# Weight sums issued behind weight slabs, and a down projection streamed by single chunks in a new order

## The chip, the core and the metric

The kernel runs on one core of one Trainium2 chip. The metric is the time of one execution on the device in microseconds. Before the change it is 2502.09 us, the median of three runs (2501.57, 2502.09 and 2509.57).

## What is computed

One layer of a transformer on 2048 tokens of width 1024 in float32: chunked softmax attention with 16 heads, each frame looking at its own 64-frame chunk and the eight before it, and then a SwiGLU network of inner width 2816. Each half is wrapped in two RMS norms.

```python
def rms_norm(x, g):
    xf = x.astype(jnp.float32)
    y = xf * lax.rsqrt(jnp.mean(xf * xf, axis=-1, keepdims=True) + RMS_EPS)
    return (y * g.astype(jnp.float32)).astype(x.dtype)
def swiglu(h, w_gate, w_up, w_down):
    return (jax.nn.silu(h @ w_gate) * (h @ w_up)) @ w_down
...
        h = rms_norm(x, g_pre_mix[i])
            m = chunk_relpos_attention(h, w_qkv[i], w_o[i], rel_bias[i // N_MIXERS])
        x = x + rms_norm(m, g_post_mix[i])
        h = rms_norm(x, g_pre_ffn[i])
        x = x + rms_norm(swiglu(h, w_gate[i], w_up[i], w_down[i]), g_post_ffn[i])
```

## The kernel before

Every float32 operand of a large product is split in two fp32r parts, a high one (ScalarE copies it, L117 and L333) and a low one (VectorE subtracts it, L118 and L334), and each product is three matmuls, high by high, high by low and low by high (L181, L182, L183).

The tokens are worked in two groups of 1024, each of two halves of 512. First come the projections of both groups with the attention between them (0 to 1115 us): weights come as slabs of 2048 columns through `fetch`, one slab ahead of its use, in two pieces of 512 KB through one buffer `raw`. Then come, for each group, gate and up (`gate_up`, 1115 to 1612 us for group 0 and 1835 to 2258 us for group 1) and down (`down`, 1612 to 1835 us and 2258 to 2484 us). These use a fast matrix multiplication in the manner of Strassen and Winograd: seven products of half size instead of eight, on sums of blocks of the activations (B11, T1 and so on) and sums of blocks of the weights (S1 to S4).

The weight sums are made once: `weight_sums` loads four blocks into tiles `ws` (four buffers), makes four additions on VectorE and stores four sums to memory. There are 17 such units, 11 for gate and up and 6 for down. They are put in `later`, a queue of steps that is worked off as the dense matmuls are written: each step has a weight, and each product of three 512-wide matmuls gives one unit of credit; `pause` is a step that does nothing.

TensorE's order is the order in which the program writes its instructions. The order on the other engines and of the DMAs issued by SyncE is set by the framework's scheduler, which may put an instruction ahead of its place in the program when its inputs and a buffer are there.

The down projection takes its operands from a stream: `ffn_ahead` loads and splits items before they are used. An item of down is a pair of the 11 chunks of 256 inner columns (the first stands alone): 512 KB of weights into one of two buffers (`raw_x`, `raw_d`), and for each chunk the activations into a scratch tile (`narrow`, nine in turn); the split activations have four buffers (tag `w4`, shared with the weights of gate and up that are loaded raw), the split weights four (`whi`, `wlo`). Items are loaded two ahead and split one ahead. Each of the seven products of down (`product`) walks all chunks, with four accumulators in PSUM; the order is B11, T1, B21, B22, T2, T3, T4 in both groups. In the last group T4 is worked twice, for 256 tokens each, so that the first half's final norm (`rstd_steps` and `finish`, put in `later` by `ended`) can run beside the second half's matmuls; its weights are loaded and split twice. The final norm of the second half of the tokens (512 wide) is put in `later` after T3, and `finish` adds the residual with eight additions, of which `share` of every four go to VectorE and the rest to GpSimd.

Of the kernel before, what the change touches and what calls it, by code (L numbers as in the profile page):

```python
# [16 lines left out]
P = 128  # L17
# [30 lines left out]
def trunk(  # L48
# [71 lines left out]
    def fetch():  # L120
# [9 lines left out]
        for c in range(2):  # L130
            here = slice(c * 1024, c * 1024 + 1024)
            if n in roomy:
                part = raw[:, here]
            else:
# [4 lines left out]
                sp.dma_start(part, plan[n][:, here])  # L139
            split_part(*tiles[c], part)  # L140
        ready.append(tiles)

    taken = [0]
# [59 lines left out]
    def pause(w):  # L203
        return [(w, lambda: None)]
# [599 lines left out]
    def weight_sums(src, dst):  # L804
# [14 lines left out]
        steps = [(0.5, lambda n=n: load(n)) for n in ("A11", "A21", "A22", "A12")] + pause(6.0)  # L819
        steps += [(2.0, lambda a=a: add(*a)) for a in sums] + pause(4.0)  # L820
# [44 lines left out]
    odd = [0]  # L865

    def down_stream(g, n, cs, c0, cols):

        a = FACTOR[n]
        m = len(cs) * HALF  # L870

        def load():
            odd[0] += 1
            if odd[0] % 2:
                raw = phase["fp"].tile([P, 1024], F32, tag="rawx", name="raw_x", bufs=1)
            else:
                raw = wp.tile([P, 1024], F32, tag="raw", name="raw_d", bufs=1)
            src = w_d[BLOCK_AT[a]] if a in BLOCK_AT else sum_d[a]
            sp.dma_start(raw[:, :m], src[:, cs[0] : cs[0] + len(cs), :].rearrange("p a b -> p (a b)"))
            cols_ = []  # L880
            for c in cs:
                cols_.append(narrow("raw_a")[:, :cols])
                sp.dma_start(cols_[-1], a_d[g][n][:, c, c0 : c0 + cols])
            return raw, cols_

        def make(got):
            raw, cols_ = got
            w = w_tile(f"d{g}_{n}_{cs[0]}_{c0}")
            split_part(w[0][:, :m], w[1][:, :m], raw[:, :m])
            acts = []  # L890
            for r in cols_:
                t = phase["fp"].tile([P, 2, HALF], F32R, tag="w4", name="a", bufs=4)
                split(t[:, 0, :cols], t[:, 1, :cols], r)
                acts.append(t)
            return w, acts

        return load, make, 2, 1


# [91 lines left out]
    def down_order(g):  # L991

        chunks = [[0]] + [[c, c + 1] for c in range(1, NC, 2)]
        for n in ("B11", "T1", "B21", "B22", "T2", "T3", "T4"):
            parts = ((0, HALF),) if n != "T4" or g < NG - 1 else ((0, HALF // 2), (HALF // 2, HALF // 2))
            for c0, cols in parts:
                for cs in chunks:
                    yield n, cs, c0, cols

    def down(g, store, between=lambda n: None):  # L1000

        p = xp.tile([P, 10, HALF], F32, tag="big", name="terms", bufs=1)
        p1, p5 = ([p[:, 4 * n + d, :] for d in range(4)] for n in range(2))

        def four(late):
# [5 lines left out]
        def product(pts, first, after):  # L1011
            for m in range(len(range(0, NC, 2))):
                (hi, lo), acts = ffn_take()
                for d in range(4):
                    for n, a in enumerate(acts):
                        cols = pts[d].shape[-1]
                        w = slice(n * HALF + d * P, n * HALF + d * P + P)
                        products(
                            pts[d], hi[:, w], lo[:, w], a[:, 0, :cols], a[:, 1, :cols],
                            first and m == 0, m == NC // 2 and n == len(acts) - 1, not first,  # L1020
                        )
                        yield 3 * C512 * cols / HALF
                    if m == NC // 2:
                        after(d)
# [428 lines left out]
```

## Time and profile before

| | us |
|---|---|
| median of three runs | 2502.09 |
| the profiled execution's own time | 2500.28 |
| its span, first to last instruction | 2498.4 |
| TensorE matmul busy in it | 2417.9 |
| VectorE busy | 1597.0 |
| ScalarE busy | 1142.5 |
| GpSimd busy | 321.2 |

Busy time of an engine counts the stretches in which at least one of its instructions ran. A wait is the idle time just before an instruction, with the instruction that released it. In the views, PE is TensorE, PEld its weight load, DVE VectorE, ACT ScalarE, POOL GpSimd and SP SyncE, which issues the DMAs; L182 is line 182 of the kernel, and a name such as `pd<-a,whi_d_T` is the output tile and the inputs. PEclk is the granted TensorE clock as a share of 2.4 GHz.

### The profile page before, as it was taken

What the parts mean: (1) busy time and instruction counts of PE and PEld (TensorE: products, weight loads), DVE (VectorE), ACT (ScalarE), POOL (GpSimd) and SP (SyncE); (2) the same over time, 40 slices, a digit from 0 to 9 for tenths busy, and PEclk for the clock granted to TensorE, in tenths of its full rate; (3) what the DMA queues carried; (4) which work ended last, traced back from release to release, by engine and by line L of the source; (5) the groups of instructions that cost most, each with busy time, mean ns of one, the idle gap of its engine ahead of it and who ended that gap; (6) DMA issues with size and microseconds to landing.
All of it is one profiled execution on the core that took longest, in us unless ns stands there. A gap on an engine that the chain in (4) does not pass through costs nothing.

```text
span 2498.4 us, 34441 instructions
## 1 busy us (share of the span) xinstructions
PE 2417.9 (97%) x12620; PEld 1998.1 (80%) x12620; DVE 1597.0 (64%) x2647; ACT 1142.5 (46%) x1930; POOL 321.2 (13%) x422
## 2 busy tenths in 40 slices
PE   7999999999999999999999999999999999999996
PEld 5787878778888888878888788788778888887885
DVE  7877775657665655568566665676556664554557
ACT  5554454654565545555333333355333323334543
POOL 4233232201222222210000000000000000000000
PEclk8999999999999999999999999999999999999998
DMA  6787861445232111147576754477667654457554
GB/s 217 276 294 282 288 238 64 156 159 168 66 100 83 62 53 62 61 137 253 166 239 215 241 178 146 154 238 244 200 204 250 219 172 149 153 180 230 191 160 160
DMA packets 176680, 444.05 MB, mean 178 GB/s; under 512 B 19424, under 2 KB 24304, under 8 KB 175232
## 3 DMA queue, kind: packets, MB, share of 16 engines
q1 hardware_dynamic: 176512, 441.87, 53.5%
q8 instruction: 99, 1.62, 0.3%
q14 instruction: 69, 0.57, 0.1%
HBM read 327.97 MB, written 113.82 MB: 177 GB/s over the span
## 4 chain that ended last, share of the span: by engine, by line
PE 46%; DMA 4%; DVE 3%; issue 2%; ACT 1%; SPq 0%; POOL 0%; DVEq 0%; POOLq 0%; ACTq 0%
PE pd L182 5%; PE pd L183 5%; PE pd L181 5%; PE pb L181 4%; PE pb L183 4%; PE pb L182 4%; PE pa L181 3%; PE pa L183 3%; PE pa L182 3%; PE pc L181 3%; PE pc L183 3%; PE pc L182 3%; DMA y<-y 1%; DMA x<-y 1%; PE mm L181 1%
## 5 line engine op out<-in xcount | busy, mean ns | idle before, releaser
L181 PE MATMUL mm<-hb,whi 128*128 128x512 f32 x720 | 299.5, 416 | 3.3 <-ACT hb L333 3.0
L531 POOL TENSOR_SCALAR sc<-sc,rows 128x640 f32<-128x640 f32 (+4 forms) x256 | 213.2, 838 | 597.6 <-DVE rows L530 561.7
L182 PE MATMUL mm<-hb,whi 128*128 128x512 f32 x720 | 285.4, 396 | 2.8 <-POOL hb L334 1.5
L527 ACT ACTIVATE sc<-sc,nmax 128x640 f32<-128x640 f32 (+4 forms) x256 | 193.8, 758 | 202.3 <-DVE nmax L523 198.0
L183 PE MATMUL mm<-hb,wlo 128*128 128x512 f32 x720 | 285.5, 397 | 0.0
L523 DVE CUSTOM_DVE_ANT_0 sc<-st,bias 128x640 f32<-128x640 f32 (+4 forms) x256 | 180.4, 737 | 82.9 <-PE st L515 76.4
L181 PE MATMUL pb<-hb,whi_gu_T 128*128 128x512 f32 x528 | 206.2, 391 | 3.9 <-DVE terms L948 3.9
L183 PE MATMUL pb<-hb,wlo_gu_T 128*128 128x512 f32 x528 | 205.5, 389 | 0.0
L182 PE MATMUL pb<-hb,whi_gu_T 128*128 128x512 f32 x528 | 205.4, 389 | 0.0
L251 POOL TENSOR_TENSOR rs<-ms,neg_half 128x4 f32<-128x4 f32 (+1 forms) x12 | 17.2, 1431 | 1279.2 <-DVE ms L249 1279.0
L334 DVE TENSOR_TENSOR a<-raw_a,a 128x512 fp32r<-128x512 f32 (+1 forms) x165 | 105.8, 653 | 109.7 <-ACT a L333 109.1
L181 PEld LDWEIGHTS mm<-hb,whi 128*128 128x128 f32 x720 | 137.0, 190 | 38.0 <-issue 14.6
L333 ACT ACTIVATE a<-raw_a 128x512 fp32r<-128x512 f32 (+1 forms) x165 | 96.6, 596 | 145.7 <-PE pd L183 115.3
L183 PEld LDWEIGHTS mm<-hb,wlo 128*128 128x128 f32 x720 | 136.8, 190 | 30.2
L182 PE MATMUL pd<-a,whi_d_T 128*128 128x512 f32 (+1 forms) x396 | 146.8, 371 | 12.7 <-DVE a L334 12.7
L182 PEld LDWEIGHTS mm<-hb,whi 128*128 128x128 f32 x720 | 137.3, 191 | 25.6 <-POOL hb L334 3.2
L181 PE MATMUL pd<-a,whi_d_T 128*128 128x512 f32 (+1 forms) x396 | 146.5, 370 | 2.0 <-ACT a L333 2.0
L183 PE MATMUL pd<-a,wlo_d_T 128*128 128x512 f32 (+1 forms) x396 | 145.8, 368 | 0.0
L181 PE MATMUL mm<-whi,hb 128*128 128x256 f32 x480 | 141.9, 296 | 0.0
L181 PE MATMUL pa<-hb,whi_gu_B 128*128 128x512 f32 x352 | 137.5, 391 | 0.1
L183 PE MATMUL pa<-hb,wlo_gu_B 128*128 128x512 f32 x352 | 137.0, 389 | 0.0
L182 PE MATMUL pa<-hb,whi_gu_B 128*128 128x512 f32 x352 | 137.0, 389 | 0.0
(222 smaller groups left out, 5898.1 us busy)
## 6 DMA issues: line engine op xcount, KB each, us to landing
raw<-gu_S SPq DMA_DIRECT2D x88, 512.0 KB, 3.7
raw<-in_w_gu SPq DMA_DIRECT2D x66, 512.0 KB, 4.0
y<-y SPq DMA_DIRECT2D x96, 256.0 KB, 4.0
ws_A<-in_w_gu SPq DMA_DIRECT2D x44, 512.0 KB, 5.7
gu_S<-ws_A SPq DMA_DIRECT2D x44, 512.0 KB, 3.0
raw<-in_w_a SPq DMA_DIRECT2D x40, 512.0 KB, 4.0
raw_a<-aT SPq DMA_DIRECT2D x77, 256.0 KB, 4.4
aT<-T SPq DMA_DIRECT2D x66, 256.0 KB, 4.1
```

Source lines behind the costliest of these rows:

```text
L181: pe.matmul(pt, a_hi, b_hi, start=first, stop=False, skip_group_check=go_on)
L182: pe.matmul(pt, a_hi, b_lo, start=False, stop=False, skip_group_check=go_on)
L183: pe.matmul(pt, a_lo, b_hi, start=False, stop=last, skip_group_check=go_on)
L251: pool.tensor_tensor(r[0][:, :nb], m[:, :nb], neg_half.to_broadcast([P, nb]), op=ALU.pow)
L333: act.activation(hi, src, AF.Copy)
L334: eng.tensor_tensor(lo, src, hi.bitcast(F32), op=ALU.subtract)
L523: dve.tensor_tensor_reduce(out=sc[:, :n], in0=st[:, c0 : c0 + n], in1=rev, scale=-1.0, scalar=3.0e38, op0=ALU.add, op1=ALU.min, accum_out= ...
L527: act.activation(sc[:, :n], sc[:, :n], AF.Exp, bias=nmax, scale=-1.0, accum_out=rows[:, 0:1])
L531: pool.tensor_scalar(sc[:, :n], sc[:, :n], rows[:, 1:2], 1.0, op0=ALU.mult, op1=ALU.mult)
```

## The change

1. The 17 units of weight sums no longer go through `later`. After the second piece of each slab 3 to 11 (group 0) and 22 to 31 (group 1) has been asked for, `fetch` writes one unit, with its loads and stores held behind that slab's DMA on SyncE's queue (`issue_after`). The pauses inside a unit are gone. So nine units stand in group 0 and eight in group 1.
2. An item of down is one chunk (256 KB of weights, 256 KB of activations, both in scratch tiles), loaded four ahead and split three ahead. The buffers `raw_x` and `raw_d` are gone.
3. In the last group the order is B11, T1, T2, T3, B22, B21, T4. T4 is walked once, 512 wide, for its first seven chunks; the last four chunks are held and worked first for 256 tokens, then for the other 256. The second half's final norm is queued after B22, with half of its additions on GpSimd.
4. Some pauses before norms change, and after the last but one attention job's output no dense work is written before the transposes that follow.

```diff
@@ fetch
-                sp.dma_start(part, plan[n][:, here])
+                ins = sp.dma_start(part, plan[n][:, here])
             split_part(*tiles[c], part)
         ready.append(tiles)
+        if units and n in UNIT_AT:
+            with tc.issue_after(ins.ins):
+                for _, step in units.popleft():
+                    step()
+    UNIT_AT = set(range(3, 12)) | set(range(22, 32))
@@ weight_sums
-        steps = [(0.5, lambda n=n: load(n)) for n in ("A11", "A21", "A22", "A12")] + pause(6.0)
-        steps += [(2.0, lambda a=a: add(*a)) for a in sums] + pause(4.0)
+        steps = [(0.5, lambda n=n: load(n)) for n in ("A11", "A21", "A22", "A12")]
+        steps += [(2.0, lambda a=a: add(*a)) for a in sums]
@@ down_stream
+            raw, cols = narrow("raw_d"), narrow("raw_a")
             src = w_d[BLOCK_AT[a]] if a in BLOCK_AT else sum_d[a]
+            sp.dma_start(raw, src[:, c, :])
+            sp.dma_start(cols, a_d[g][n][:, c, :])
...
-        return load, make, 2, 1
+        return load, make, 4, 3
@@ down, product
+            for m in range(NC - tail):
+                item = ffn_take()
                 for d in range(4):
+                    yield part(item, m, d, whole)
+            items = []
+            for here in parts:
+                for d in range(4):
+                    for m in range(tail):
+                        if len(items) == m:
+                            items.append(ffn_take())
+                        yield part(items[m], NC - tail + m, d, here)
+                    after(d, here)
+                between_parts(here)
@@ down, the last group
+        yield from product(pc, False, c22)
+        if end:
+            yield from product(pb, False, c12)
+            between(0)
+            p2 = four()
+            yield from product(p2, True, lambda d, _: store(0, d, whole, add(p2[d], p1[d])))
+        p4 = four(not end)
         yield from product(
+            p4, True, lambda d, here: store(0, 4 + d, here, add(p4[d][:, here], u3[d][:, here])),
+            (slice(0, HALF // 2), slice(HALF // 2, HALF)) if end else (whole,), 4 if end else 2,
         )
@@ dense
-                        later.extend(sp1[:4] + near[:1] + sp1[4:] + near[2:] + last.write(0.7))
+                        later.extend(sp1[:4] + near[:1] + sp1[4:] + pause(5.0) + near[2:] + last.write(0.7))
...
-                g, 0, preps[0].load(w=1.5) + pause(3.0) + preps[0].rstd() + pause(1.0) + preps[0].norm(), 4
+                g, 0, preps[0].load(w=1.5) + pause(6.0) + preps[0].rstd() + pause(1.0) + preps[0].norm(), 4
@@ ended
+                post = post_of(*((1, slice(0, HALF)), (0, slice(0, N)), (0, slice(N, HALF)))[n])
+                wait, w, share = ((4.0, 2.0, 2), (1.0, 0.5, 3), (0.0, 0.0, 2))[n]
+                if n:
+                    drain()
+                later.extend(pause(wait) + rstd_steps(post.total, post.total, 5.0) + post.finish(w, share))
@@ the attention loop
-                jobs[t // 4 - 1].output()
                 i = t // 4 - 1
-                fill(0.2 * rate)
+                jobs[i].output()
+                fill(0.2 * rate if i < 2 * NPAIR - 2 else 0.0)
```

## Rows read from the trace of the kernel before

**Rows 1.** Page, busy time of each engine, TensorE's row

```profile
PE 2417.9 (97%) x12620; PEld 1998.1 (80%) x12620; DVE 1597.0 (64%) x2647; ACT 1142.5 (46%) x1930; POOL 321.2 (13%) x422
```

**Rows 2.** Windows by stage: length, busy us per engine, PEclk, DMA share, GB/s

```profile
0.00:60.00 60.00, 42.78 (x198) 32.32 (x199) 43.14 (x49) 31.78 (x53) 23.80 (x28) 0.89 0.60 213
60.00:360.00 300.00, 288.19 (x1787) 237.35 (x1786) 237.66 (x464) 159.98 (x332) 96.82 (x126) 0.99 0.80 286
360.00:600.00 240.00, 229.68 (x1285) 187.69 (x1283) 153.74 (x309) 133.69 (x255) 48.12 (x70) 0.99 0.39 132
600.00:1115.00 515.00, 509.85 (x3284) 425.00 (x3286) 306.99 (x663) 276.94 (x525) 137.99 (x188) 1.00 0.24 78
1115.00:1612.00 497.00, 494.08 (x2205) 407.86 (x2201) 319.80 (x425) 189.75 (x261) 5.35 (x4) 1.00 0.61 197
1612.00:1835.00 223.00, 217.10 (x946) 176.74 (x946) 144.81 (x197) 106.09 (x160) 0.00 (x0) 1.00 0.71 232
1835.00:2258.00 423.00, 421.89 (x1873) 349.19 (x1872) 250.28 (x325) 141.19 (x183) 3.38 (x2) 1.00 0.59 190
2258.00:2430.00 172.00, 170.36 (x743) 140.10 (x742) 86.81 (x111) 78.44 (x118) 0.00 (x0) 0.99 0.61 193
2430.00:2484.00 54.00, 42.84 (x309) 41.15 (x307) 45.32 (x87) 23.43 (x45) 1.70 (x2) 0.91 0.53 170
2484.00:2498.40 14.40, 1.14 (x8) 0.71 (x6) 8.42 (x21) 1.19 (x3) 4.09 (x5) 0.69 0.31 106
```

**Rows 3.** Additions of the weight sums: by form, 60 to 360 us; all

```profile
L813 DVE TENSOR_TENSOR ws_A<-ws_A,ws_A 128x1024 f32<-128x1024 f32 x60 | 77.4, 1289 | 14.9 <-DMA ws_A<-in_w_gu 7.9 <-DMA ws_A<-in_w_d 5.5 <-DVE nmax L523 0.8
L813 DVE TENSOR_TENSOR ws_A<-ws_A,ws_A x68: 686/1225/1709, 40.6 to 358.2; 128x1024 f32<-128x1024 f32 x64, 128x512 f32<-128x512 f32 x4
```

**Rows 4.** Timeline, TensorE: start, duration, instruction, [idle before it]; before 1115 us

```profile
488.71 0.50 PE L181 MATMUL py<-hb,whi 128*128 128x512 f32 x1 [1.22 <-ACT hb L333]
...
527.92 1.05 PE L247 MATMUL pssq<-ones,prep 128*128 128x1 f32 x8 [1.97 <-DVE prep L233]
...
600.55 0.65 PE L263 MATMUL prs<-ident,rs 128*128 128x128 f32 x4 [3.19 <-POOL rs L251]
...
1090.97 0.49 PE L181 MATMUL py<-hb,whi 128*128 128x512 f32 x1 [0.70 <-ACT hb L333]
```

**Rows 5.** Timeline, TensorE: two waits in the first group's down

```profile
1615.08 0.49 PE L181 MATMUL pd<-a,whi_d_B 128*128 128x512 f32 x1 [1.50 <-ACT a L333]
...
1816.73 0.49 PE L181 MATMUL pd<-a,whi_d_T 128*128 128x512 f32 x1 [1.04 <-ACT a L333]
```

**Rows 6.** Windows of the last T4, and the longest wait there in the timeline

```profile
2457.00:2462.00 5.00, 0.70 (x6) 0.50 (x5) 5.00 (x11) 0.97 (x3) 0.00 (x0) 1.00 0.57 187
2462.00:2472.00 10.00, 5.72 (x27) 5.72 (x28) 7.75 (x13) 1.93 (x4) 0.70 (x1) 0.50 0.73 241
2472.00:2484.00 12.00, 12.00 (x100) 11.93 (x99) 10.37 (x25) 5.41 (x12) 0.00 (x0) 0.99 0.30 98
...
2466.28 0.58 PE L182 MATMUL pd<-a,whi_d_T 128*128 128x256 f32 x1 [8.58 <-DVE a L334]
```

**Rows 7.** Groups by form, 1612 to 1835 us: the splits of down on VectorE

```profile
L334 DVE TENSOR_TENSOR a<-raw_a,a 128x512 fp32r<-128x512 f32 x76 | 51.3, 689 | 38.4 <-ACT a L333 38.4
...
L118 DVE TENSOR_TENSOR wlo_d_T<-raw_d,whi_d_T 128x1024 fp32r<-128x1024 f32 x12 | 14.7, 1225 | 8.3 <-ACT whi_d_T L117 8.3
```

**Rows 8.** DMA issues: count, KB each, median us from issue to landing; weights of down

```profile
raw_d<-in_w_d SPq DMA_DIRECT2D x21, 512.0 KB, 3.8
...
raw_x<-in_w_d SPq DMA_DIRECT2D x7, 256.0 KB, 4.3
```

**Rows 9.** Timeline of the end: the last large matmul, and final scalings on VectorE

```profile
2483.85 0.28 PE L183 MATMUL pd<-a,wlo_d_T 128*128 128x256 f32 x1
...
2488.49 0.88 DVE L375 SCALAR_TENSOR_TENSOR hb<-hb,gt,total 128x256 f32<-128x256 f32 x2 [1.50 <-ACT total L264]
...
2489.95 2.60 DVE L375 SCALAR_TENSOR_TENSOR hb<-hb,gt,total 128x256 f32<-128x256 f32 x4
```

More of the change, by code (lines that the diff above doesn't have):

```diff
@@ L991, in down_order, with four @@
     def down_order(g):
[L993 to L998, printed above, removed]
+        return ("B11", "T1", "B21", "B22", "T2", "T3", "T4") if g < NG - 1 else (
+            "B11", "T1", "T2", "T3", "B22", "B21", "T4")
     def down(g, store, between=lambda n: None):
+        end = g == NG - 1
         p = xp.tile([P, 10, HALF], F32, tag="big", name="terms", bufs=1)
         p1, p5 = ([p[:, 4 * n + d, :] for d in range(4)] for n in range(2))
-        def four(late):
+        whole = slice(0, HALF)
+        def four(late=False):
             return [
@@ L1009, in four, with product, part @@
             ]
-        def product(pts, first, after):
-            for m in range(len(range(0, NC, 2))):
-                (hi, lo), acts = ffn_take()
-                for d in range(4):
[L1015 to L1024, printed above, removed]
+        def product(pts, first, after, parts=(whole,), tail=2):
+            def part(item, m, d, here):
+                hi, lo, a = item
+                w = slice(d * P, d * P + P)
+                products(
+                    pts[d][:, here], hi[:, w], lo[:, w], a[:, 0, here], a[:, 1, here],
+                    first and m == 0, m >= NC - tail - 1, not first or m >= NC - tail,
+                )
+                return 3 * C512 * (here.stop - here.start) / HALF
+            for m in range(NC - tail):
+                item = ffn_take()
+                for d in range(4):
+                    yield part(item, m, d, whole)
[8 more added lines that the diff above has]
+                between_parts(here)
@@ L1045, in u @@
+        pc = four()
+        def u(d, _):
+            if not end:
+                u2[d] = narrow("u2")
             dve.tensor_tensor(u2[d], pc[d], p1[d], op=ALU.add)
         yield from product(pc, True, u)
-        for d in range(4):
-            store(1, d, 0, HALF, add(pb[d], u2[d]))
-        def c22(d):
-            dve.tensor_tensor(p1[d], pc[d], p1[d], op=ALU.add)
-            store(1, 4 + d, 0, HALF, add(p1[d], p5[d]))
-        yield from product(pc, False, c22)
-        between(0)
-        if g < NG - 1:
-            pe_ = four(True)
-            yield from product(pe_, True, lambda d: store(0, 4 + d, 0, HALF, add(pe_[d], p1[d])))
-            return
@@ L1061, in down, with c12, c22 @@
-        for part in range(2):
-            c0, cols = part * HALF // 2, HALF // 2
-            pe_ = [b[:, :cols] for b in four(part == 0)]
-            yield from product(
-                pe_, True,
-                lambda d: store(0, 4 + d, c0, cols, add(pe_[d], p1[d][:, c0 : c0 + cols])),
-            )
-            between(1 + part)
+        def c12(d, _):
+            store(1, d, whole, add(pb[d], u2[d]))
+        if not end:
+            for d in range(4):
+                c12(d, 0)
+        def c22(d, _):
+            dve.tensor_tensor(u3[d], pc[d], p1[d], op=ALU.add)
+            store(1, 4 + d, whole, add(u3[d], p5[d]))
@@ L1216, in dense @@
                     continue
[L1217 to L1219 removed]
                 if g == NG - 1 and p == 2:
[L1221 to L1223 removed]
+                    later.extend(blocks[0].sums(8.0))
                 for s in range(2):
@@ L1327, in trunk @@
     phase["psa"] = stack_a.enter_context(tc.tile_pool(name="psa", bufs=2, space=PSUM))
+    units.extend(gate_up_sums(c) for c in range(NC))
+    units.extend(down_sums(c) for c in [0] + list(range(1, NC, 2)))
     work = dense()
```

90 lines of the change are left out of this document (33 added, 57 removed).

## The prediction, made before the changed kernel ran

> **What bounds the kernel now.** I read the page's busy times first: TensorE is busy for 2417.9 of the 2498.4 us of the span, so 80.5 us at most can be had without touching the matmuls [rows 1]. Then the windows by stage, where length less TensorE's busy time is the idle time of a stage [rows 2]. It is 17.2 us in the first 60 us, 11.8 in 60 to 360, 10.3 in 360 to 600, 5.2 in 600 to 1115, 2.9 in the first group's gate and up, 5.9 in its down, 1.1 in the second gate and up, 1.6 in most of the second down, 11.2 in the last product and 13.3 in the tail after the last large matmul. Each stage is TensorE's with small holes, and every term below is a hole that closes or opens, or matmuls that become slower or fewer. I took the holes one by one in the timeline and the groups by form for the work beside them.
>
> **Weight sums (part 1).** All 68 additions ran between 40.6 and 358.2 us, the six units of down among them, although the program writes those far later [rows 3]. So in the program before, their credits did not pace them; buffers did. In 60 to 360 us they cost VectorE 60 x 1.289 = 77.4 us [rows 3], of its 237.7 us busy in 300, which is 79% [rows 2]. From 600 to 1115 us, with no sums, VectorE is 60% busy and TensorE idles 5.2 us, of which 3.2 is one wait on a norm [rows 2, 4]: 2.0 us in 515, or 1.2 in 300. So at most 11.8 - 1.2 = 10.6 us of the first stretch belongs to the sums. The change holds a unit's loads behind a slab, so nine units spread over group 0 and eight over group 1: nine units are 46 us of additions instead of 77, and over some 320 us that takes VectorE's load from 79% to about 68% in the first; eight units, 41 us, raise it from 60% to 68% in the second. The bounds: all 10.6 us go, or they move with the units (0.62 us each over 17) and nothing is gained. Nothing in the trace shows a unit on its own in a quiet stretch. Holes on a queue shrink faster than its load, but the work stays; I take the middle, **-5 us**. DMAs are no bound: eight units load and store 32 MB, which over 515 us adds 65 GB/s to the 78 of that stretch, and 286 flowed in the first [rows 2]. Queued behind the unit's loads on SyncE are the next slab and the attention's small loads and stores; the next slab needs buffers that come free only when one more slab is used up, so I cost the stores that wait for the additions at nothing; if they hold SyncE, that is the second rival.
>
> **Pauses and the empty fill (part 4).** TensorE waits 1.97 us at 527.92 for a sum of squares and 3.19 us at 600.55 for a power [rows 4]. Three and five more credits, each of three matmuls of about 0.23 us (421.89 us over 1873 in the second gate and up [rows 2]), put 2.0 and 3.4 us of matmuls in front: both close, unless the chains also end later. **-4.5** of 5.2. The o projection's first matmul waits 1.22 and 0.70 us for the split of the last attention output [rows 4]; with no dense work written there, the next job's transposes come first and cover it. **-1.5** of 1.9.
>
> **Single chunks, deeper stream (part 2).** The waits in the first group's down come at its beginning (1.50 us) and where its buffers are shared with the next gate and up (1.04 us) [rows 5], the rest after product starts: a pair's split activations need two of four `w4` buffers, which the last pair of the product before gives up only at its end. Released by the chunk and split three ahead (3 x 12 x 0.225 = 8.1 us instead of one pair, 5.4 us, or one single, 2.7 us), they should mostly go: **-4.5** of 5.9, and **-1.2** of the 1.6 at the start of the second [rows 2]. The price is on other engines: a pair's low part took 1.225 us on VectorE, two single ones take 2 x 0.689 = 1.38 [rows 7]: 5 x 0.15 us in each product, beside 29.8 us of matmuls; nothing on the path while VectorE has 35% free in that stage [rows 2]. If the cover went, 14 products would cost 11 us.
>
> **The last group (part 3).** In the last T4 TensorE waits 8.58 us for a low part of activations, while VectorE is busy without a break: 5.00 of 5.00 us [rows 6]. It does the 512-wide final norm ahead of the split. All of the stretch's 11.2 us of idle time [rows 2] are such waits. Behind the wait the granted clock is 0.50, which is 1.2 GHz, for ten microseconds: 27 matmuls in 5.72 us there, 100 in 12.00 us after it [rows 6], so 27 x (0.212 - 0.120) = 2.5 us lost. One 512-wide walk over seven chunks saves 84 x (2 x 0.120 - 0.225) = 1.3 us. Together 15.0 us to be had. After the change the wide norm starts a product earlier, with B21 and T4 behind it, and VectorE also loses the second split of T4's weights. Its work in those two products, by durations: 2 x 11 x 1.38 = 30 for splits, 8 scalings and 4 additions of about 0.7 = 8, stores and squares 10, up to 4 more because GpSimd now adds beside it (four scalings took 2.60 us beside GpSimd at the end, two took 0.88 alone [rows 9]): 52 of about 60 us. It fits, with little room. New costs: the four held chunks fill all four split buffers, so the last of them can be split only after the chunk before the four is done, two low parts of 0.689 us [rows 7] and the copies ahead of them, some 2.0 us, against three half-width products, 9 x 0.120 = 1.1 us: 1.2 us with a margin; 0.4 us for the first half's sum of squares, which now stands behind few matmuls; 1 us for VectorE's lag. Net **-12.4**. The tail after the last large matmul is 2498.4 - 2483.85 = 14.5 us [rows 9]. The second half's matmuls shrink from 132 to 48, 5.8 us, so the first half's eight scalings and six additions (256 wide, about 5.5 us) no longer fit beside them; part of that overlaps the second half's chain of sum, power and transposes. **+2**, between 0 and +5.5.
>
> **The sum:** -5 - 4.5 - 1.5 - 4.5 - 1.2 - 12.4 + 2 = -27.1, on the profiled execution's 2500.3 us: 2473. That execution was 1.8 us under the median of 2502.1; I keep **2473** for the median, since the gain is made of waits that vary little from run to run.
>
> **Rivals.** (a) The holes move. The sums give nothing (+5), the tail takes its 5.5 us (+3.5), half of down's waits return at other places (+3): 2485. For it: the order on VectorE is a scheduler's and one late instruction shifts many. Against it: the largest hole, 8.58 us, has its cause written in the program. (b) Slower, through VectorE's order. Written at the slab, a unit's four additions (4 x 1.289 = 5.2 us) now stand ahead of the attention work that the program writes after it, while before they filled gaps. If x us of each burst reaches TensorE, the sum is -27.1 + 5 - 10.6 + 17x, zero at x = 1.9; at 2.5 it is 2510. Now it is 0.62 us per unit at most. (c) Slower, through supply. A 256 KB load lands after 4.3 us, a 512 KB load after 3.8 [rows 8], so half the bytes take no less time. If SyncE or the scratch ring holds the loads so that each chunk needs 0.3 us more than its 2.7 us of matmuls, 154 chunks cost 46 us and down's gains of 5.7 are lost: 2525. It decides once landing and splits (about 4.4 + 2.0 us) pass the four chunks of lead, 10.8 us, so after 4.4 us of delay. The Trainium skill, page "DMA: Bandwidth & Descriptors", section "Rules for kernel authors", asks for transfers of at least 1 MiB and for coalescing small ones, which speaks against this part; the rows on landing agree that small loads are no quicker, but the share of 0.71 shows no full queue. (d) The change does not do what it says: the sums still run early and the last product still waits for VectorE. Then part 4 and the 1.3 us of fewer matmuls remain, -7.3: 2493, and up to 2500 if those fall too. (e) Better: the sums' whole 10.6 us go and the tail does not grow: 2465 and less.
>
> **How the numbers follow.** Forecast (2466 to 2480) 0.48, (a) 0.22, (d) 0.10, (e) 0.10, (b) 0.06, (c) 0.04. A measurement of this kernel tells about 0.3%, 7.5 us, from no change, so 2494.6 and 2509.6 are the borders: faster 0.48 + 0.22 + 0.10 and a few hundredths from the quick end of (d), 0.82; slower 0.08, since part of (b) stays within the border; same 0.10. The range leaves out (b), (c) and the slower end of (d): 2456 to 2496. Its lower end is all holes of the sums gone (-5.6), no growth of the tail (-2), both first terms of part 4 and down whole (-2.9), no lag in the end (-2.6) and some of the 360 to 600 us stretch.
>
> **What would show it.** Right: additions of the sums from about 80 us to 1000 us; TensorE's idle time in 60 to 360 us near 7 us; the waits at 528 and 600 us gone; first down under 2 us idle; the last product without a wait over 2 us and at clock 1.00 until its end; a tail of 15 to 18 us. Wrong: a wait of several us for VectorE in B21 or T4, a clock of 0.50 there, waits behind the additions in 600 to 1000 us, or ScalarE waiting for `raw_d` and `raw_a` loads all through down.

## The result, and the profile after

Medians: 2502.1 us before, 2488.2 after; ratio 0.9943, 95% interval 0.9919 to 0.9966. The change is faster by some 14 us. The time lies in the range of the forecast, but the gain is less than half of the 29 us that it put. The profiled execution of after took 2493.5 us, with a span of 2491.6.

The windows of both kernels, cut at the first matmul of each stage (projections and attention; gate and up; down; the same for the second group, its last down ending with the last large matmul; tail). Columns as in [rows 2]; length less TensorE's busy time is its idle time. Before:

```profile
20.00:1182.50 1162.50, 1128.62 (x6830) 932.28 (x6831) 781.23 (x1541) 618.47 (x1189) 296.49 (x397) 0.99 0.45 156
1182.50:1610.70 428.20, 425.33 (x1898) 351.77 (x1897) 264.59 (x351) 156.62 (x211) 5.35 (x4) 1.00 0.59 188
1610.70:1829.10 218.40, 212.50 (x926) 172.95 (x925) 143.90 (x196) 105.17 (x160) 0.00 (x0) 1.00 0.70 229
...
2252.30:2483.90 231.60, 218.80 (x1075) 185.95 (x1073) 135.81 (x203) 102.88 (x162) 1.70 (x2) 0.97 0.60 190
2483.90:2498.40 14.50, 1.24 (x8) 0.74 (x7) 8.52 (x22) 1.22 (x3) 4.09 (x5) 0.69 0.31 108
```

After:

```profile
20.00:1195.70 1175.70, 1134.13 (x6829) 938.40 (x6830) 778.50 (x1543) 621.32 (x1190) 292.20 (x397) 0.99 0.44 154
1195.70:1624.50 428.80, 426.70 (x1897) 353.01 (x1897) 265.31 (x353) 157.11 (x213) 5.36 (x4) 1.00 0.59 188
1624.50:1834.80 210.30, 210.00 (x925) 173.31 (x924) 144.20 (x226) 107.70 (x189) 0.00 (x0) 1.00 0.71 232
...
2258.00:2472.20 214.20, 212.81 (x989) 177.62 (x988) 131.14 (x209) 99.81 (x176) 12.96 (x6) 1.00 0.60 194
2472.20:2491.60 19.40, 1.71 (x10) 1.01 (x9) 12.32 (x30) 1.10 (x3) 5.58 (x7) 0.62 0.31 109
```

The two down stages became 8.1 and 17.4 us shorter, the tail 4.9 longer, and the attention stage 13.2 longer where 11 less were forecast: 7.7 us more idle time and 5.5 more for the same matmuls. The additions now run from 90 to 927 us, against 40.6 to 358.2 [rows 3] (first line: shortest, median and longest in ns), and TensorE's longest waits in that stage are on VectorE (the other lines: total, times, longest, from 20 to 1170 us):

```profile
L820 DVE TENSOR_TENSOR ws_A<-ws_A,ws_A x68: 673/1222/1630, 90.4 to 927.4; 128x1024 f32<-128x1024 f32 x64, 128x512 f32<-128x512 f32 x4
...
PE st L521 <- DVE nmax L530: 14.5, 10, 2.7
PE pssq L254 <- DVE total L240: 5.9, 1, 5.9
```

In before, the scores' products (`st`) had 2.5 us of such waits for the maximum (`nmax`). The windows of [rows 2] show where the idle time grew:

```profile
60.00:360.00 300.00, 289.84 (x1806) 240.28 (x1805) 200.38 (x434) 159.85 (x334) 84.33 (x125) 0.99 0.50 181
...
600.00:1115.00 515.00, 498.53 (x3188) 415.69 (x3186) 335.13 (x683) 271.55 (x513) 141.27 (x185) 0.99 0.39 137
```

From 60 to 360 us VectorE is busy for 37 us less than before, and TensorE's idle time fell only from 11.8 to 10.2 us. From 600 to 1115 us, where before had no sums, it rose from 5.2 to 16.5. The longest single wait has its cause on the queues. On SyncE a column (`sum`) of the second group's norm is issued behind a slab and the unit's four loads; on VectorE its addition into `total` stands behind additions of the unit:

```profile
861.14 0.33 SPq L139 DMA_DIRECT2D raw<-in_w_a  x1
861.52 2.04 SPq L817 DMA_DIRECT2D ws_A<-in_w_d  x4
863.68 0.38 SPq L703 DMA_DIRECT2D sum<-x  x1
...
870.27 2.48 DVE L820 TENSOR_TENSOR ws_A<-ws_A,ws_A 128x1024 f32<-128x1024 f32 x2
...
873.41 1.22 DVE L820 TENSOR_TENSOR ws_A<-ws_A,ws_A 128x1024 f32<-128x1024 f32 x1
874.54 0.68 DVE L240 TENSOR_TENSOR total<-total,sq 128x512 f32<-128x512 f32 x1
...
875.28 1.02 PE L254 MATMUL pssq<-ones,total 128*128 128x1 f32 x4 [5.85 <-DVE total L240]
```

### The profile page after: what moved, and what is told of

It is laid out like the page before. It is cut to its first block, busy times and chain, and to the rows that moved or that the text cites. A ratio compares the mean times of both kernels' runs of the same rounds, so it can differ in the third digit from the quotient of the medians.

```text
span 2491.6 us, 34707 instructions
## 1 busy us (share of the span) xinstructions
PE 2418.1 (97%) x12536; PEld 1998.1 (80%) x12536; DVE 1595.5 (64%) x2698; ACT 1145.0 (46%) x1979; POOL 328.7 (13%) x428
## 4 chain that ended last, share of the span: by engine, by line
PE 52%; DMA 1%; DVE 1%; issue 0%; ACT 0%; POOL 0%; SPq 0%; POOLq 0%; DVEq 0%; ACTq 0%
PE pd L189 5%; PE pd L188 5%; PE pd L190 5%; PE pb L188 5%; PE pb L189 5%; PE pb L190 5%; PE pa L188 3%; PE pa L189 3%; PE pa L190 3%; PE pc L188 3%; PE pc L189 3%; PE pc L190 3%; PE mm L188 1%; PE mm L190 1%; PE mm L189 1%; DMA res<-in_x 1%
## 5 line engine op out<-in xcount | busy, mean ns | idle before, releaser
L538 POOL TENSOR_SCALAR sc<-sc,rows 128x640 f32<-128x640 f32 (+4 forms) x256 | 204.3, 802 | 595.5 <-DVE rows L537 545.8
L521 PE MATMUL st<-k,q 128*128 128x384 f32 (+1 forms) x448 | 132.5, 316 | 17.3 <-DVE nmax L530 14.5
L188 PE MATMUL mm<-whi,hb 128*128 128x256 f32 x480 | 143.4, 299 | 0.0
L189 PE MATMUL pd<-a,whi_d_T 128*128 128x512 f32 (+1 forms) x368 | 140.0, 380 | 0.7 <-DVE a L341 0.7
L188 PE MATMUL pd<-a,whi_d_T 128*128 128x512 f32 (+1 forms) x368 | 140.1, 381 | 0.1
L190 PE MATMUL pd<-a,wlo_d_T 128*128 128x512 f32 (+1 forms) x368 | 139.8, 380 | 0.0
L190 PE MATMUL mm<-whi,hb 128*128 128x256 f32 x480 | 136.7, 285 | 0.0
```

The lines of the kernel that those rows point to most:

```text
L188: pe.matmul(pt, a_hi, b_hi, start=first, stop=False, skip_group_check=go_on)
L189: pe.matmul(pt, a_hi, b_lo, start=False, stop=False, skip_group_check=go_on)
L190: pe.matmul(pt, a_lo, b_hi, start=False, stop=last, skip_group_check=go_on)
L521: pe.matmul(st[:, a:b], q[:, h, cols], kk[:, h, key], start=True, stop=False)
L538: pool.tensor_scalar(sc[:, :n], sc[:, :n], rows[:, 1:2], 1.0, op0=ALU.mult, op1=ALU.mult)
```

## The experiments

In the list, a unit is tied when it is written at its slab and its loads are held behind that slab's DMA; its additions stand in gaps when they go through `later` and run early, as in before; they are paced when only the loads are tied and the additions follow from the list at a set number of products. Runs e3, e5, e11, e12 and e13 leave out part of the sums' work and so compute another output.

Medians of four to twelve executions each; the ratio is to the kernel before in the same session. The kernel before had medians from 2498.7 to 2502.1 us in these sessions, so a difference of 2 or 3 us between runs says nothing.

| run | us | ratio, 95% |
|---|---|---|
| after | 2488.2 | 0.9943 [0.9919, 0.9966] |
| e1 sums in gaps | 2472.3 | 0.9888 [0.9868, 0.9907] |
| e2 before + ties | 2515.8 | 1.0068 [1.0046, 1.0089] |
| e3 no sums | 2458.5 | 0.9833 [0.9813, 0.9853] |
| e4 column 5.0 | 2486.3 | 0.9941 [0.9922, 0.9960] |
| e5 tied loads and stores | 2495.2 | 0.9980 [0.9968, 0.9992] |
| e13 tied loads | 2459.1 | 0.9835 [0.9811, 0.9859] |
| e12 tied loads, additions | 2487.7 | 0.9950 [0.9932, 0.9967] |
| e11 additions, early | 2464.7 | 0.9858 [0.9836, 0.9881] |
| e10 halves | 2516.0 | 1.0066 [1.0040, 1.0092] |
| e15, e19 paced 4, 6.5 | 2477.0, 2471.5 | 0.9906 [0.9890, 0.9922], 0.9891 [0.9874, 0.9908] |
| e18 at output projection | 2509.0 | 1.0040 [1.0025, 1.0056] |
| e20 mixed | 2475.3 | 0.9900 [0.9886, 0.9915] |
| e6, e7 GpSimd: tied, gaps | 2542.8, 2538.1 | 1.0168 [1.0144, 1.0192], 1.0155 [1.0133, 1.0177] |
| e8 gaps, tail | 2473.0 | 0.9894 [0.9873, 0.9914] |
| e14 gaps, no pauses | 2478.3 | 0.9909 [0.9893, 0.9925] |
| e17 gaps, old order | 2481.1 | 0.9916 [0.9903, 0.9930] |

**e1: the ties alone undone,** and with them the missing pauses inside a unit.

```diff
-        steps = [(0.5, lambda n=n: load(n)) for n in ("A11", "A21", "A22", "A12")]
-        steps += [(2.0, lambda a=a: add(*a)) for a in sums]
+        steps = [(0.5, lambda n=n: load(n)) for n in ("A11", "A21", "A22", "A12")] + pause(6.0)
+        steps += [(2.0, lambda a=a: add(*a)) for a in sums] + pause(4.0)
...
+                if g == 0 and p == 1:
+                    for c in range(NC):
+                        later.extend(gate_up_sums(c))
                 if g == NG - 1 and p == 2:
                     later.extend(blocks[0].sums(8.0))
+                    for c in [0] + list(range(1, NC, 2)):
+                        later.extend(down_sums(c))
...
-    units.extend(gate_up_sums(c) for c in range(NC))
-    units.extend(down_sums(c) for c in [0] + list(range(1, NC, 2)))
```

> The kernel after with its first part alone undone: the 68 additions of the weight sums, their loads and their stores stand again in the list of steps and run early in the gaps of VectorE, as in the kernel before; the single chunks, the new order of the last group and the longer pauses stay. Theory (the ties cost: untied, the additions filled gaps; tied, they stand as ordinary work among attention's VectorE chain and put 2 MB of loads ahead of small ones): from the profiles the stages behind attention gain 20.6 us in the kernel after (-8.1, -17.4, +4.9) and attention loses 13.2, so this run is below the kernel after: 2470 to 2482, and gate-up of the first group starts near 1180 us instead of 1195.7. Rival (the loss comes from the other edits of the attention stage, the pauses and the heavier column sums): 2486 to 2492, gate-up starting near 1195. My forecast's own step (the ties gain 5 us): above the kernel after, near 2493.

2472.3: 15.9 us below after, and faster than both kernels. **e2**, the same lines the other way round in the kernel before:

> The kernel before with the first part alone: the units of the weight sums tied behind slabs, without their pauses; everything else as before. Theory (the ties cost): slower than before by 5 to 13 us, 2507 to 2515, and gate-up of the first group starts 5 to 13 us later than 1182.5. Rival (the ties are harmless or a gain, and the loss of the kernel after comes from the pauses and the heavier column sums): 2495 to 2502, gate-up starting at or before 1182.5. The forecast's step says 2497.

2515.8, 15.5 over before in the same session. Two different kernels around the ties, one price: the ties (part 1 as a whole) lose some 15 us, and the other edits of the attention stage, the pauses of part 4 among them, are not to blame.

**e3: no sums at all** (no units; the loads read `w_gu[c, BLOCK_AT.get(a, 0)]`, and `w_d` likewise).

> The kernel after without the weight sums at all: no loads, additions or stores of S1 to S4; the products that read them read an original block of the same size instead (so the output is another one). It shows what the sums cost wherever they stand. Theory: the sums in the gaps cost little, so this is 0 to 8 us below the run that puts them back into the gaps, 2465 to 2480, and gate-up of the first group starts at 1172 to 1182 us. Rival (the attention stage of the kernel after is long for another reason): gate-up still starts at or after 1190, 2482 to 2490.

2458.5. So the sums cost 29.7 us as after has them and 13.9 in the gaps, more than the 0 to 8 I expected. The attention stage without sums, with sums in the gaps (e1), beside after, above:

```profile
20.00:1155.40 1135.40, 1121.07 (x6830) 931.72 (x6831) 702.47 (x1474) 618.02 (x1189) 272.81 (x397) 1.00 0.29 99
```

```profile
20.00:1175.10 1155.10, 1125.47 (x6827) 932.37 (x6827) 779.84 (x1542) 619.06 (x1190) 296.87 (x397) 0.99 0.45 157
```

Idle time 14.3, 29.6 and 41.6 us; busy time 1121, 1125 and 1134 us for the same matmuls, with the granted clock at 1.00, 0.99 and 0.99. Of the 40 us between e3 and after, 27 are waits and 13 are matmuls that take longer between them. These 40 are of two single executions; the medians differ by 29.7, because the profiled execution of after was 5.3 us over its median and the later stages of e3's took 5.9 us longer.

**e4: the long wait alone** (`blocks[0].sums(8.0)` to `sums(5.0)`, which puts the last column's load ahead of the unit's; the change had also raised this weight from 5.0, which the description of the change leaves out).

> The kernel after with one number changed: the weight of the second group's column sums is 5.0 as before, not 8.0, which puts the last column's load ahead of the four loads of the weight-sum unit that it stood behind. Theory (the single pause of 6.0 us at 869 us comes from the column load behind 2 MB of weight loads): the pause goes, gate-up starts 5 to 13 us earlier (1183 to 1190), 2476 to 2484. Rival (VectorE's order alone, or a pause that only moves): 2486 to 2492, with a wait of the same kind at another place.

2486.3, a ratio of 0.9941 beside 0.9943: the time is the rival's. The wait of 5.9 us fell to 0.4, but the scores' waits stayed, at 14.9 us. Gate and up did begin at 1188.8 us, as the theory had it, but beside a profiled execution of after that was 5.3 us over its median. The striking wait was not what the ties cost.

**e5: additions left out** (the line that adds the four additions to `steps` is deleted).

> The kernel after with the additions alone left out: the tied units still load four blocks behind their slab and store four tiles (unsummed, so the output is another one); the same bytes move at the same places. It parts the sums' cost into transfers and VectorE. Theory (the additions on VectorE delay attention's chain): near the run without any sums, which took 2458.5 us and began gate-up at 1155.4: 2458 to 2466, gate-up at 1155 to 1163, PE idle between 20 us and gate-up 14 to 20 us. Rival (the 2 MB in and 2 MB out per unit hold the queue and the engines' small loads): 2480 to 2488, gate-up at 1182 or later, PE idle over 32 us.

2495.2, worse than with the additions. My first theory, that the additions on VectorE are the whole cost, falls here as it was put. The reason shows on SyncE:

```profile
719.03 1.96 SPq L817 DMA_DIRECT2D ws_A<-in_w_d  x4
727.29 2.92 SPq L828 DMA_DIRECT2D d_S<-ws_A  x4
730.26 1.18 SPq L420 DMA_DIRECT2D bias<-ext_d  x1
...
736.87 0.14 POOL L421 MEMSET bias<- 64x64 f32 x1 [5.51 <-DMA bias<-ext_d]
...
737.25 0.82 DVE L530 CUSTOM_DVE_ANT_0 sc<-st,bias 128x640 f32<-128x640 f32 x1 [6.21 <-POOL bias L422]
...
738.14 0.69 PE L521 MATMUL st<-k,q 128*128 128x384 f32 x1 [7.21 <-DVE nmax L530]
```

The stores now come right behind the loads and hold the queue for 6.3 us until the data is there; the bias behind them is late, and TensorE waits 7.2 us. VectorE's waits for the bias were 22.0 us in this run, 3.2 in after. So this is a second way to lose, opened by the experiment itself. The next three take it apart; in their texts A is VectorE's order and B the stores at the head of SyncE's queue.

**e13, e12, e11.** e13 deletes additions and stores, e12 the stores alone (both read original blocks, as e3); e11 loads four blocks once and adds on them.

> The kernel after with only the loads of the weight sums: no additions, no stores (another output). Beside the run with loads and stores (2495 us) it leaves the stores out alone. B (the stores hold SyncE's queue while they wait for the loads to land): 2458 to 2465, waits of GpSimd and VectorE for the bias back to 26 and 2 us. C (2 MB of loads in one burst delay the small loads behind them by themselves): 2468 to 2490, with the bias still late.

2459.1, 0.6 us over e3: here tied loads cost nothing that can be measured.

> The kernel after with the stores of the weight sums left out: loads and additions stay where they are tied, the products read original blocks (another output). B (stores at the head of SyncE's queue): 2458 to 2468, gate-up before 1168. A (VectorE's order): as the run with additions alone, 2478 to 2490. If both cost, each run lies between, and this one above the one with additions alone.

2487.7: with the additions, the whole price is back (28.6 us), and after's stores add nothing to it that can be measured (0.5 us). Theory B is out for after, A is in; between e13 and e12 the only edit is the 68 additions.

> The kernel after with the transfers of the weight sums left out: four blocks are loaded once, by the first unit, and all 68 additions run on them at the tied places; nothing is stored, and the products read original blocks (another output). Two theories are open, since the run without the additions lost as much as the kernel after (2495 us against 2458.5 without any sums). A, VectorE's order: additions ahead of the scores' maximum and of the copies of the transposes stop PE: 2478 to 2490 here, gate-up from 1175 to 1195. B, SyncE's queue: a unit's four stores wait at its head for their data (104 us of such waits in the kernel after, 83 in the run without additions) and hold the loads of the bias and of columns behind them: here 2458 to 2464, gate-up from 1155 to 1161.

2464.7, but the test missed its aim: without loads to wait for, the additions were ordered early, 83.6 to 249.4 us, so the run says only that 68 additions in gaps, without transfers, cost 6.2 us. Whether the rest of e1's 13.9 comes with the transfers or with the other places of its additions is not shown.

**What an addition does.** One place of after and the same place of e3, the two maxima of a job (VectorE, then TensorE). After:

```profile
392.92 1.23 DVE L820 TENSOR_TENSOR ws_A<-ws_A,ws_A 128x1024 f32<-128x1024 f32 x1
394.06 0.82 DVE L530 CUSTOM_DVE_ANT_0 sc<-st,bias 128x640 f32<-128x640 f32 x1
394.80 0.08 DVE L530 DVE_READ_ACCUMULATOR2_ANT nmax<- 128x1 f32 x1
394.80 1.22 DVE L820 TENSOR_TENSOR ws_A<-ws_A,ws_A 128x1024 f32<-128x1024 f32 x1
395.94 0.16 DVE L537 RECIPROCAL rows<-rows 128x1 f32<-128x1 f32 x1
396.01 0.81 DVE L530 CUSTOM_DVE_ANT_0 sc<-st,bias 128x640 f32<-128x640 f32 x1
...
396.88 0.33 PE L521 MATMUL st<-k,q 128*128 128x128 f32 x1 [2.58 <-DVE nmax L530]
```

e3:

```profile
379.09 0.82 DVE L530 CUSTOM_DVE_ANT_0 sc<-st,bias 128x640 f32<-128x640 f32 x1
379.84 0.08 DVE L530 DVE_READ_ACCUMULATOR2_ANT nmax<- 128x1 f32 x1
379.84 0.82 DVE L530 CUSTOM_DVE_ANT_0 sc<-st,bias 128x640 f32<-128x640 f32 x1
...
380.72 0.33 PE L521 MATMUL st<-k,q 128*128 128x128 f32 x1 [0.25 <-DVE nmax L530]
```

An addition stands ahead of each maximum: two of 1.2 us, and the wait grows from 0.25 to 2.58.

**e15 and e19: the ties kept, the additions paced.**

```diff
-                for _, step in units.popleft():
+                unit = units.popleft()
+                for _, step in unit[:4]:
                     step()
+            later.extend(unit[4:])
...
-        steps += [(2.0, lambda a=a: add(*a)) for a in sums]
+        steps += [(4.0, lambda a=a: add(*a)) for a in sums]
```

> The kernel after with only the four loads of a unit tied to its slab; its four additions and four stores go into the list of steps, one addition for every four products of a projection, so that they can't run before their loads nor stand in one bunch. Theory (a bunch of four additions, one ahead of each of attention's VectorE steps, is what costs): waits of the scores' products on the maximum fall from 14.5 us to under 8, 2468 to 2481, against 2487.7 with loads and additions in a bunch and 2458.5 without sums. Rival (each addition costs its 0.4 us of PE wherever it stands in the attention stage, as two halves cost twice as much): 2484 to 2492, no change.

> The paced run (2477.0 us) with one addition for every 6.5 products of a projection in place of 4. Theory (bunches cost): the four additions of a unit run over 8 us and more instead of a median of 6.4, waits of the scores' products on the maximum fall below 10.6 us; 2468 to 2474. Rival (the spread has done what it can; what is left is the additions' own 85 us on VectorE inside attention): 2475 to 2480. A third: the later stores and loads push other steps of the list back: above 2480.

2477.0 and, with 6.5 in place of 4.0, 2471.5: 11 and 17 us below after, with the same loads, additions and stores. From the start of a unit's first addition to that of its last is 4.9, 6.1 and 6.8 us (medians of 17) in after, e15 and e19, and the sums cost 29.7, 18.5 and 13.0. TensorE's waits for the maximum, 14.5 us in after, in e15 and then in e19:

```profile
PE st L523 <- DVE nmax L532: 10.6, 7, 2.8
...
PE st L523 <- DVE nmax L532: 4.7, 6, 1.5
```

So the four additions bunched at the slab are what cost, and placing them otherwise takes that cost away. What it is about the bunch stays open: pacing spreads the additions and also writes them behind attention steps that after writes later, and spread and order were not parted. I had expected under 8 us of these waits in e15 and 8 us of spread in e19; neither came. Paced, the sums cost what they cost in gaps (13.0 and 13.9), not less.

**e10: halves** (each addition as two of 512 columns).

> The kernel after with each addition of 1024 columns as two of 512: the same work on VectorE in pieces half as long. A, if the length of one piece is what attention's steps wait for: 2472 to 2482. A, if the sum of the pieces counts, or B: 2484 to 2495, no change.

2516.0, slower still, against every theory. 132 pieces cost 57.5 us over e3, 68 cost 29.7: 0.44 us each in both, so in these two runs the price went with the number of pieces and not with their length. The bunches did not grow for it (4.2 us from first to last start). Why is open.

**e18 and e20: other places** (`UNIT_AT = set(range(3, 20))`, which moves the second group's eight units, two of gate and up and six of down, to the output projection; and gate-up's eleven units in the gaps with down's six paced).

> The kernel after with the eight units of down's sums tied behind the eight slabs of the first group's output projection (510 to 640 us, where no scores are made until its end) in place of slabs of the second group's attention. Theory (the price of an addition is that it stands ahead of attention's steps): the second group's attention goes back to the pace of the run without sums (PE waits there under 8 us, the bursts from 652 to 1125 us close up by 10 to 18 us), the output projection grows by at most 5; 2474 to 2482. Rival (the additions cost the same anywhere): 2485 to 2492, the loss moved into 510 to 640 us.

2509.0. The second group's attention did recover (windows of e18: 4.3 us of idle time in 460; after had 14.2 in 473), but the output projection paid: 27.7 us idle in 170, where after had 3.5 in 139, one wait of 17.4 us on the next group's sum of squares among it. I had put 5 us. This wait is not of the additions alone: the last two columns of the next group (`prep`) were asked for behind a slab and the unit's four loads, and ScalarE waited for them, so here the place of the tied loads has its part.

```profile
510.00:680.00 170.00, 142.25 (x757) 121.31 (x756) 123.04 (x181) 74.15 (x124) 19.56 (x23) 0.91 0.71 260
680.00:1140.00 460.00, 455.71 (x2905) 376.30 (x2903) 272.89 (x598) 252.53 (x480) 128.71 (x174) 1.00 0.23 74
...
PE pssq L254 <- DVE prep L240: 22.2, 2, 17.4
...
586.18 3.12 SPq L817 DMA_DIRECT2D ws_A<-in_w_d  x4
589.36 0.98 SPq L290 DMA_DIRECT2D prep<-in_x  x2
...
597.37 1.27 ACT L239 ACTIVATE sq<-prep 128x512 f32<-128x512 f32 x2 [3.90 <-DMA prep<-in_x]
```

> The nine units for gate-up in the gaps of the first group, as in the kernel before, and the eight for down tied and paced in the second. Theory (each group's attention has gaps for some additions, and the price rises with their number): below both the run with all in the first group's gaps (2472.3) and the paced one (2477.0), 2464 to 2470. Rival (the price is per addition, 0.2 us in the gaps and 0.27 paced): 36 x 0.2 + 32 x 0.27 over 2458.5, 2473 to 2476.

2475.3: the rival. With the eleven and six units that the edit makes, not nine and eight, its sum is 2458.5 + 44 x 0.2 + 24 x 0.27 = 2474. Nothing is won by sharing the sums between the groups.

**e6 and e7: additions on GpSimd**, tied and in the gaps (`dve.tensor_tensor` to `pool.tensor_tensor`).

> The kernel after with the additions on GpSimd in place of VectorE, tied as they were. GpSimd is busy some 290 of the 1175 us of the attention stage. Theory (what costs is an addition standing in VectorE's queue ahead of the scores' maximum): waits of the scores' products on the maximum fall from 14.5 us to under 4; but GpSimd also scales every block of scores, 0.80 us each, so a longer addition there would show as waits of the transposes on GpSimd; 2462 to 2480 if those stay under 10 us. Rival (transfers are the cost): no better than the kernel after, 2484 to 2495, with the scores' products still waiting.

> The run with the sums back in the gaps (2472.3 us), with the additions on GpSimd in place of VectorE. Theory (VectorE's order is the cost in the gaps as well; without any sums the time is 2458.5): 2460 to 2470, with PE idle before gate-up falling from 29.6 us towards 14.3. Rival (GpSimd's additions delay its scaling of the scores as much as VectorE's delayed the maximum): 2472 to 2485, waits of the transposes on GpSimd over 10 us.

2542.8 and 2538.1, above every range that I had put: the transposes now wait for GpSimd's scaling of the scores (28.4 and 46.6 us). In e7 the waits for the maximum fell to 1.1 us; in e6, where I had put under 4, they rose from 14.5 to 19.0. GpSimd also finishes the bias, and VectorE waited 28.9 us for it in e6, against 3.2 in after. So e6 does not clear VectorE's order; it opens a third way to lose. An addition takes twice as long on GpSimd (first line), and the maximum in e6:

```profile
L820 POOL TENSOR_TENSOR ws_A<-ws_A,ws_A x68: 1276/2400/3135, 88.7 to 976.0; 128x1024 f32<-128x1024 f32 x64, 128x512 f32<-128x512 f32 x4
...
PE st L521 <- DVE nmax L530: 19.0, 7, 6.0
```

2.40 against 1.22 us, 1.96 times. The Trainium skill, page "GPSIMD Engine Reference", section "Elementwise — side-by-side cycle accounting", has the same 1.96 for an fp32 addition of 2048 elements; this case agrees, at 1024.

**e8: the tail.** `ended(2)` runs the first step of its root ahead of `drain()`.

> The run with the sums back in the gaps (2472.3 us), and one step of the tail moved: the sum over the second half's columns and its root are given out ahead of the first half's scalings and additions, not behind them. In the kernel after the sums of squares of the second half were there at 2474.4, their VectorE step ran at 2479.1 behind ten steps of the first half, and PE waited 5.8 us for GpSimd. Theory (the tail is VectorE's order): the tail after the last product falls from 19.5 us to 14 to 17, the time to 2467 to 2471, and that wait of PE to under 3 us. Rival (the tail is the length of the finish, 16 scalings and 16 additions, whatever their order): 2471 to 2474, tail unchanged.

The wait did go, from 5.8 to 1.3 us, but the tail went only from 19.7 us in e1 (19.4 in after) to 18.3, and the time stayed at 2473.0: the rival. VectorE is busy for 12.8 of those 18.3 us:

```profile
2452.70:2471.00 18.30, 1.49 (x11) 0.95 (x9) 12.82 (x30) 1.10 (x3) 5.88 (x7) 0.64 0.33 115
```

**e14 and e17: single terms, on e1.** e14 takes out the pauses, the 8.0 and the empty fill; e17 puts the old order of the last group back.

> The run with the sums back in the gaps (2472.3 us), with the edits of the attention stage undone as well: the pauses of 5.0 and 6.0, the weight 8.0 of the column sums and the empty fill at the last job but one; only the down stage and the tail differ from the kernel before. The forecast's terms: pauses -4.5 and fill -1.5, so 6 us slower than that run, 2476 to 2481, gate-up starting near 1182.5 as before, and the waits of 1.97 us at 528 and 3.19 us at 600 back. Rival (the pauses do nothing): 2470 to 2474.

2478.3, 6.0 over e1 by the medians, as forecast, but of four and five executions whose intervals overlap; in the profiles the attention stage is only 1.6 us longer than e1's (1156.7 and 1155.1). The wait of 3.2 us at 600 us is back, the one of 1.97 at 528 is not (0.8).

> The run with the sums back in the gaps (2472.3 us), with the last group's products in the old order (B21, B22, T2, T3, T4, the last split into column parts as in the kernel after) on single chunks. It parts the two edits of the last down stage, which together took it from 231.6 to 214.2 us. The forecast's term: the order gains 12.4 net, so 2482 to 2487, with the wait of some 8.6 us ahead of the last product's second half or its stand-in back. Rival (the single chunks and the tail of four chunks did it, not the order): 2472 to 2476, the stage at 214 to 218 us.

2481.1, 8.8 over e1. The last down stage (the profiled execution was 10.4 us over the median; this stage takes 214 us in the profiles of after, e1, e3 and e19 alike):

```profile
2244.90:2470.20 225.30, 218.32 (x988) 182.33 (x987) 129.59 (x205) 101.97 (x180) 10.52 (x6) 0.97 0.57 184
```

225.3 us beside 231.6 before and 214.2 after: in the profiles the order gave 11.1, and the rest of the edit in this stage (single chunks, the four held ones, half of the norm's additions on GpSimd) gave 6.3. The long wait had shrunk in the old order too: of the 8.58 us ahead of the second half of T4 [rows 6], waits of at most 1.9 were left, and one of 3.2 for a norm's sum.

## Why the prediction came out as it did

**Weight sums, -5: wrong, and in sign.** By e1 and e2 the ties cost 15 to 16 us. The step that failed is "Holes on a queue shrink faster than its load", with its two bounds, of which the worse was that nothing is gained: I priced VectorE by its load per stretch (79% to 68%), and that did fall, to 200.4 of 300 us in after's 60 to 360 against 237.7 [rows 2]. TensorE's idle time there should have come near 7 us and was 10.2; from 600 to 1115 us, where VectorE's load rose from 60% to 65% and eight units could cost 5.0 us at most by my 0.62 each, it rose by 11.3. What the runs showed in place of load is where an addition stands. In before, the additions were ordered into gaps; at the slab they stand ahead of attention's steps, and the pauses of the unit were gone. The 68 additions alone are the price (e13 to e12, 28.6 us), and moving them out of the bunch takes up to 17 us back (e19). This was rival (b), which I gave 0.06; its x, the price of a unit, is 29.7 / 17 = 1.75 us, against 13.9 / 17 = 0.82 in the gaps (I had at most 0.62). The point from which (b) decides, 1.9, was nearly reached; the sums of before cost 13.9 us and not the 10.6 that (b) takes off, and other terms came out better, and that kept the change faster.

**Stores and loads on SyncE at nothing:** right for after (0.5 and 0.6 us, nothing that can be measured), though e5 shows 36 us once stores stand right behind their loads. I did not cost the heavier column sums; e4 puts them at 1.9 us, nothing that can be measured.

**Pauses, -4.5: about right; fill, -1.5: not got.** The wait at 600 us is gone and the one at 528 became 0.9, so 4.3 of the 5.2 us went. The o projection's waits (`py`) did not close: 2.7 us in all in before (first two lines), 3.0 in after. At the second place the wait of 0.70 us for the high part went, and one of 0.71 for the low part came.

```profile
PE py L181 <- ACT hb L333: 1.9, 2, 1.2
PE py L182 <- DVE hb L334: 0.8, 2, 0.5
...
PE py L189 <- DVE hb L341: 2.0, 2, 1.3
PE py L188 <- ACT hb L340: 1.0, 1, 1.0
```

The 6.0 of e14 is of the forecast's size, but not clear of noise, and it doesn't bear out the fill.

**First down, -4.5:** 5.9 us of idle time became 0.3, as argued; 2.5 us less busy time was not foreseen, so -8.1. Rival (c) did not come: chunks of 256 KB landed after 3.5 to 4.1 us (medians). The Trainium skill, page "DMA: Bandwidth & Descriptors", section "Rules for kernel authors", asks for at least 1 MiB per DMA for the highest bandwidth. This stage, with weight loads of 256 KB in place of 512, got 8.1 us shorter. Smaller loads and the deeper stream came together and were not parted.

**Last group, -12.4 and -1.2 at its start:** -17.4 in the profile: 11.4 us less idle time and 6.0 less busy time. No wait over 1 us is left there and the clock is 1.00. By e17 the order gave 11.1 of it (8.8 by the medians), near its net, and the rest 6.3, more than the start and the fewer matmuls (1.2 and 1.3). Of the 2.6 us of new costs little shows. So the wait of 8.58 us did not need the new order to shrink.

**Tail, +2:** +4.9, near the upper bound. The first half's finish does not overlap the second's chain: VectorE holds that chain's step until 2479.1. With that step put first (e8) the tail still took 18.3 us; what fills it was not taken apart.

**The sum again.** Without the ties the terms gave 22.1 by forecast; before to e1 is 28 us (2500.3 to 2472.3). Less 15 to 16 for the ties that leaves 12 to 13; measured, 14. That e1 sits at my 2473 is chance: one term was wrong by 20 us, the others short by 6. That after lies in my range is in part the same luck: the 6 us too little made up for some of the 20.

## What to carry to other kernels

In this kernel an engine's load in a stretch did not price the work that moved onto it; ask ahead of which steps the moved work will stand in its queue, and who waits for those. Loads tied behind attention's slabs were free here (behind the output projection's they held up others), and the four additions bunched behind them were not: tie the load where nothing small waits behind it, and pace the work. And when an experiment takes work away, look at what moves up into its place (e5, e11) before reading the time.

## What the runs showed of the hardware that I had not expected

- Cutting VectorE's pieces in half made the stage longer, not shorter (29.7 us over e3 for 68 pieces, most of 1.22 us, and 57.5 for 132 of 0.68; 0.44 per piece in both).
- A third of the loss in the attention stage, 13 of 40 us, is matmuls that take longer between the waits and not the waits themselves (busy time 1121.1 to 1134.1 us, granted clock 1.00 to 0.99).
- SyncE held a unit's first store for 6.3 us until its data was there, while a small load that attention needed stood behind the four stores, and TensorE waited 7.2 us (e5). With the stores gone (e13), VectorE's waits for that load fell from 22.0 us to none.
